# Pausing the adaLN steps in the SSM and MLA part, moving the rotary keys' PSUM read to ScalarE, and giving GpSimd some of the weights' low parts

## The chip, the core and the metric

The kernel runs on one core of one Trainium2 chip. The metric is the device time of one launch in microseconds (us); the time before is the median of three runs. The engines are named as in the profile: PE (matmul), DVE (VectorE), ACT (ScalarE), POOL (GpSimd), SP (SyncE, which here only issues DMAs).

## The reference, cut to what matters

A trunk of two layers over 512 tokens of width 1024. A layer is FFN, token mixer, FFN, each modulated by adaLN columns and followed by a LayerNorm. The mixer has three branches that read the same input:

```python
DEPTH = 2; SEQ = 512; D_MODEL = 1024
ada = (cond @ w_ada[l] + b_ada[l]).reshape(B, 3, 3, D)          # shift, scale, gate of each sub-layer
...
proj = h @ w_in + b_in
q_a, kv_a, k_rope, dil_qkv, u, gate_logits = jnp.split(proj, SPLIT_POINTS, axis=-1)
k_pe = jnp.broadcast_to(rope(k_rope, positions)[:, :, None, :], (B, S, MLA_HEADS, MLA_ROPE_DIM))
y_mla = causal_block_attention(q, k, kv[..., MLA_NOPE_DIM:], ...)  # latent attention (MLA), 8 heads
y_dil = dilated_attention(qkv[:, :, 0], qkv[:, :, 1], qkv[:, :, 2])
y_ssm = jax.nn.gelu(s5_ssm(u, lam_re, lam_im, log_dt, b_re, b_im, c_re, c_im, d_skip))
y_ssm = y_ssm * jax.nn.sigmoid(y_ssm @ w_glu + b_glu)
merged = (gates[:, :, 0] * (y_mla @ w_br[0]) + gates[:, :, 1] * (y_dil @ w_br[1]) + gates[:, :, 2] * (y_ssm @ w_br[2]))
return merged @ w_out
```

## The kernel before, in words

**Weights.** Every large product is done in three f32r matmuls on high and low parts: `wh*xh + wh*xl + wl*xh` (`mm3`, L129 to L131). A chunk of four 128x128 weight tiles comes in by one SP DMA of 256 KB (`wraw`), ACT casts it to its high part (`whi`, L110), and DVE, or POOL while `self.share` is set and the chunk's number is odd, subtracts to the low part (`wlo`, L112). Chunks are numbered through the program; numbers 146 to 180 of layer 0 are the ones spoken of here, 604 and up in layer 1.

**adaLN.** The adaLN matrix isn't multiplied on PE: each column block `araw` is loaded by SP and reduced on DVE (`ada_col`, L183, one custom instruction of 128x512 and a small read of the accumulator). The blocks are spread over the program as jobs: `tick` takes one job from `self.jobs` each time it is called.

**Who sets the order.** The Python order is a priority. A list scheduler with its own cost table places the instructions of each engine's queue; each engine then runs its queue strictly in order and waits at semaphores.

**The mixer's first part** (some 430 to 500 us of layer 0 and 1875 to 1945 us of layer 1) runs four SSM chains `ssm_f` (f = 0 to 3), with the low-rank projections of MLA (`low_rank`) and the dilated values as filling. For each f:

- `ssm_powers` builds the matrices `W` and `C` on POOL by complex products (`cmul`, L536 to L541, 128x64 each), with a scratch tile from `half`;
- ACT copies them into block form (`BD` and `CD`, L697 and L699);
- PE transposes and multiplies them (L732, L739), ACT copies the results (`BT` L734, `T` L743);
- DVE turns the input by phases and scans (`Z` L755 to L760, L765, L767 to L772), and PE takes the result (L779);
- later DVE and ACT compute the gelu (`y` L790, `t` L791 to L794, with a load of an activation table).

In `low_rank`, five products are read out of PSUM by ACT as `raw0` to `raw4` (L1117); the sixth holds the rotary keys, which DVE reads out of PSUM as `kpe` (L1128).

**A shared scratch.** `half` has six buffers that are used in turn (128x256). Among the users are the POOL products of `ssm_powers`, the DVE phases (`ssm_phases`) and four loads of a permutation table for the dilated part (L1241), which are issued as DMAs from ACT's queue:

```python
    def half(self):
        return self.t(self.sb, "half", 6, 256)
...
                for z in range(4):
                    sl = slice(256 * z, 256 * z + 256)
                    pz = self.half()
                    nc.scalar.dma_start(pz, self.A["perm"][:, sl])      # L1241
                    nc.scalar.copy(self.perm[:, sl], pz)
```

A load of the table can be issued once the earlier user of its buffer is done. In Python these loads stand after the MLA part; the scheduler places them earlier, inside the SSM part.

Of the kernel before, what the change touches and what calls it, by code (L numbers as in the profile page):

```python
# [12 lines left out]
AF = mybir.ActivationFunctionType  # L13
ALU = mybir.AluOpType
# [27 lines left out]
class Packer:  # L42


    def __init__(self):
        self.tiles = []
        self.ada = []


class Builder:  # L50
    def __init__(self, nc, tc, ctx, A, pk, plan):
        self.nc, self.tc, self.A, self.pk, self.plan = nc, tc, A, pk, plan
        ep = ctx.enter_context

        self.edge = ep(tc.tile_pool(name="edge", bufs=1, side="right"))
        self.edge.tile([P, 56], F32, name="edge")
        self.const = ep(tc.tile_pool(name="const", bufs=1))
        self.wp = ep(tc.tile_pool(name="wp", bufs=1))
        self.sb = ep(tc.tile_pool(name="sb", bufs=1))
        self.hs = tc.tile_pool(name="hs", bufs=1, space=bass.MemoryType.DRAM)  # L60
        self.hs = ep(self.hs)
        self.ps = ep(tc.tile_pool(name="ps", bufs=8, space=PSUM))
        self.ntile = 0
        self.nada = 0
        self.cur = None
        self.share = False
        self.normed = None
        self.jobs = iter(())
        self.gated = set()
        self.side = iter(())  # L70
        self.uid = 0
# [118 lines left out]

    def tick(self, n=1):
        for _ in range(n):
            next(self.jobs, None)
            with self.behind():
                next(self.side, None)

# [912 lines left out]
    def low_rank(self, p, l, out):  # L1109


        nc = self.nc
        raw = []
        for n in range(5):
            ps = self.gemm([("w_in", (l,), k, n) for k in range(KT)], self.x)
            r = self.t(p, f"raw{n}")
            nc.scalar.activation(r, ps, AF.Identity, bias=self.col(("b_a", l), n))  # L1117
            raw.append(r)
            if n == 2:
                rq = self.rms(l, raw[:3], "q_norm", 384)  # L1120
                next(rq)
            yield
        next(rq)
        rr = 640 + np.arange(32)
        sw = 640 + (np.arange(32) + 16) % 32
        ps = self.gemm([("w_in", (l,), k, np.concatenate([rr, sw, rr, sw])) for k in range(KT)], self.x)
        kpe = self.t(p, "kpe")
        nc.vector.scalar_tensor_tensor(kpe, ps, self.col(("b_kr", l)), self.rope, ALU.add, ALU.mult)  # L1128
        yield
        rk = self.rms(l, raw[3:], "kv_norm", 256)  # L1130
        next(rk)
        yield
        next(rq, None)
        next(rk)
        yield
        ps = self.pst()
        ks = self.t(self.sb, "sq", 2)[:, :P]
        nc.scalar.dma_start(ks, self.A["kpe_sum"])
        nc.tensor.matmul(ps, ks, kpe, start=True, stop=True)
        nc.scalar.copy(kpe, ps)  # L1140
        yield
        next(rk, None)
        kvn = []
        for r in raw[3:]:
            kvn.append(self.pair(p, f"kv{len(kvn)}"))
            self.split(r, *kvn[-1])
        out.update(q=raw[:3], kvn=kvn, kpe=kpe)

    def mixer(self, l, nxt, last, pend):
        nc = self.nc  # L1150
# [3 lines left out]
        def drain(g):  # L1154
            for _ in g:
                pass
        with self.pool("r") as rp:
            with self.pool("u") as up, self.pool("ssm") as sp:
                us = self.project(up, l, pend)
                lr = {}  # L1160

                def values():
                    for g in range(3):
                        for r in self.dil_values(sp, l, g):
                            if r is not None:
                                Vd[g] = r
                            yield
                low = self.low_rank(rp, l, lr)
                val = values()

                def side_work():
                    for _ in range(6):
                        yield next(low)
                    for _ in range(4):
                        next(low, None)
                        yield next(val)
                    yield from val
                fill = side_work()
                chains = [self.ssm_f(sp, l, f, us[f]) for f in range(4)]
                y_ssm = []  # L1180
                glu = self.glu(self.sb, sp, l, us, y_ssm)
                step(chains[0])
                drain(self.ssm_powers(l, 1))
                step(fill)
                step(fill)
                self.ssm_blocks(1)
                for f in range(4):
                    step(chains[f])
                    if f > 0:
                        drain(chains[f - 1])  # L1190
                    if f < 3:
                        self.ssm_phases(f + 1)
                    for _ in range(FILLS[f][0]):
                        step(fill)
                    if f < 3:
                        step(chains[f + 1])
                        if f < 2:
                            drain(self.ssm_powers(l, f + 2))
                    for _ in range(FILLS[f][1]):
                        step(fill)  # L1200
                    step(chains[f])
                    for _ in range(FILLS[f][2]):
                        step(fill)
                    if f < 2:
                        self.ssm_blocks(f + 2)
                drain(fill)
                step(glu)
                drain(chains[3])
                drain(glu)
            self.prep_pool.__exit__(None, None, None)  # L1210
            with self.pool("mla") as mp:
                parts = []
                for r in lr["q"]:
                    parts.append(self.pair(mp, f"n{len(parts)}"))
                    self.split(r, *parts[-1])
                self.mla_mask = self.table(mp, "mla_mask", S)
                for r in self.mla_prepare(mp, l, lr["kvn"], lr["kpe"]):
                    if r is not None:
                        Ks, Vs = r
                y_mla, yb = [], {}  # L1220

                hs = [self.mla_head(mp, l, h, parts, Ks[h], Vs, yb) for h in range(8)]

                for h in range(-3, 9):
                    if h + 3 < 8:
                        step(hs[h + 3])
                    if h >= 2 and h % 2 == 0:
                        y_mla.append(self.mla_values(h // 2 - 1, Vs, yb))
                    if 0 <= h < 8:
                        drain(hs[h])  # L1230
                    if -2 <= h < 6:
                        step(hs[h + 2])
        with self.pool("yd") as yp:
            y_dil = []
            pre = []
            with self.pool("dil") as dp:
# [26 lines left out]
                for hh in range(4):  # L1263
# [2 lines left out]
                        for _ in range((2, 1, 1, 2, 0)[k]):  # L1266
                            step(fill)
                    drain(fill)
            self.tick(99)
            with self.pool("merge") as p:  # L1270
                return self.merge(p, l, (y_ssm, y_mla, y_dil), pre, nxt, last)

# [7 lines left out]
    def merge(self, p, l, ys, pre, nxt, last):  # L1280

        nc = self.nc
        acc = [self.t(p, f"acc{n}") for n in range(KT)]
        for bi, br in enumerate((2, 0, 1)):
            parts = []
            for k, y in enumerate(ys[bi]):
                parts.append(self.pair(p, f"y{k}"))
                self.split(y, *parts[-1])
            for n in range(KT):
                sg = pre[n] if bi == 0 and n < len(pre) else self.gate(p, l, br, n, "sg", 3)  # L1290
                ps = self.gemm([("w_br", (l, br), k, n) for k in range(4)], parts)
                if bi == 0:
                    nc.vector.tensor_tensor(acc[n], sg, ps, ALU.mult)
                else:
                    nc.vector.tensor_tensor(sg, sg, ps, ALU.mult)
                    nc.vector.tensor_tensor(acc[n], acc[n], sg, ALU.add)
        merged = []
        for n in range(KT):
            merged.append(self.pair(p, f"m{n}"))
            self.split(acc[n], *merged[n])  # L1300
        self.new_h()
        for j in range(KT):
            nc.scalar.dma_start(self.H[j], self.hd[j])
        return self.tail(lambda n: [("w_out", (l,), k, n) for k in range(KT)], merged, self.mod[l, 1][2], nxt, last)
# [187 lines left out]
```

## Time and profile before

| what | value |
| --- | --- |
| time before, median of 3 runs | 2906.31 us (2905.78 to 2906.53) |
| profiled execution: its own time | 2904.84 us |
| profiled execution: span from first to last instruction | 2902.7 us |
| mean granted TensorE clock | 0.982 of full speed |
| PE busy in the span | 2804.4 us (97%) |
| DVE / ACT / POOL busy | 1671.0 / 1109.5 / 467.8 us |

The times in the trace are those of the profiled execution, counted from its span's start. PE is nearly always busy, so a change can only win where PE waits, and it loses wherever it makes PE wait more. The matmuls of a 128x512 tile start every 0.22 to 0.23 us at full clock.

### The profile page before, as it was taken

The page shows a single profiled execution, that of the slowest core. Times are in us where ns is not written, and L with a number is a line of the kernel's source. Part 1 is how long each engine was busy: PE and PEld are TensorE (multiplying, and loading weights), DVE is VectorE, ACT ScalarE, POOL GpSimd, SP SyncE. Part 2 cuts the span into 40 slices and gives each one's busy share as a digit, 9 for nine tenths or more (in the row PEclk, how much of TensorE's full clock was granted, in tenths as well). Part 3 has the DMA queues.
Part 4 walks back from the last instruction along what each step waited for, and adds up shares of the span by engine and source line. Part 5 has one row for each costly group of instructions (what it writes and reads, how often), then busy time and mean ns, then how long its engine had stood idle before and what let it go on. Part 6 is the DMA issues. An engine that isn't in the chain of part 4 may idle for free.

```text
span 2902.7 us, 40766 instructions
## 1 busy us (share of the span) xinstructions
PE 2804.4 (97%) x14384; PEld 2375.5 (82%) x14384; DVE 1671.0 (58%) x4234; ACT 1109.5 (38%) x2174; POOL 467.8 (16%) x728
## 2 busy tenths in 40 slices
PE   8999998999999989999999999989999999999997
PEld 6888886978888878888888888869788888888886
DVE  8755469983444465544566554699734444753334
ACT  4333244373443334223343233543643433432332
POOL 2120375000000060000421003840000000600004
PEclk9999999999999999999999999989999999999998
DMA  7545345543234324544244453446422343153331
GB/s 278 168 134 146 112 122 161 184 147 98 84 91 113 98 63 141 153 120 147 87 118 141 135 145 102 145 135 203 142 84 81 97 113 97 58 160 102 96 98 51
DMA packets 205836, 359.38 MB, mean 124 GB/s; under 512 B 23104, under 2 KB 40000, under 8 KB 205632
## 3 DMA queue, kind: packets, MB, share of 16 engines
q1 hardware_dynamic: 198864, 346.32, 39.9%
q10 hardware_dynamic: 6768, 10.47, 1.2%
q8 instruction: 112, 1.84, 0.3%
q14 instruction: 92, 0.75, 0.1%
HBM read 339.92 MB, written 16.78 MB: 123 GB/s over the span
## 4 chain that ended last, share of the span: by engine, by line
PE 84%; DVE 8%; POOL 3%; DMA 2%; ACT 2%; issue 1%; ACTq 0%; DVEq 0%; SPq 0%; POOLq 0%
PE ps L129 26%; PE ps L130 26%; PE ps L131 26%; PE ps L899 1%; DVE wlo L112 1%; DMA araw<-wa 1%; DMA wraw<-ws 1%; DVE lnst L148 1%; DVE araw L183 1%; PE ps L1090 1%; DVE lnst L147 1%; PE ps L316 1%; PE ps L1002 1%; PE ps L1079 0%; PE ps L931 0%
## 5 line engine op out<-in xcount | busy, mean ns | idle before, releaser
L110 ACT CAST whi<-wraw 128x512 fp32r<-128x512 f32 x916 | 563.6, 621 | 1287.8 <-PE ps L130 925.4
L112 DVE TENSOR_TENSOR wlo<-wraw,whi 128x512 fp32r<-128x512 f32 x872 | 608.3, 702 | 733.9 <-ACT whi L110 707.4
L130 PE MATMUL ps<-xl,whi 128*128 128x512 f32 (+1 forms) x2496 | 943.6, 378 | 0.3 <-DVE xl L139 0.3
L129 PE MATMUL ps<-xh,whi 128*128 128x512 f32 (+1 forms) x2496 | 940.0, 379 | 3.3 <-ACT xh L136 3.2
L131 PE MATMUL ps<-xh,wlo 128*128 128x512 f32 (+1 forms) x2496 | 941.6, 378 | 0.0
L129 PEld LDWEIGHTS ps<-xh,whi 128*128 128x128 f32 x2496 | 472.1, 190 | 88.6 <-ACT xh L136 5.0
L131 PEld LDWEIGHTS ps<-xh,wlo 128*128 128x128 f32 x2496 | 472.7, 189 | 85.2
L130 PEld LDWEIGHTS ps<-xl,whi 128*128 128x128 f32 x2496 | 473.3, 190 | 84.2 <-DVE xl L139 0.5
L129 PE MATMUL ps<-gh,whi 128*128 128x512 f32 (+1 forms) x836 | 304.0, 364 | 0.3 <-ACT gh L136 0.3
L130 PE MATMUL ps<-gl,whi 128*128 128x512 f32 (+1 forms) x836 | 301.6, 361 | 0.2 <-DVE gl L139 0.2
L131 PE MATMUL ps<-gh,wlo 128*128 128x512 f32 (+1 forms) x836 | 300.6, 360 | 0.0
L112 POOL TENSOR_TENSOR wlo<-wraw,whi 128x512 fp32r<-128x512 f32 x44 | 58.4, 1328 | 1165.1 <-ACT whi L110 1165.1
L130 PEld LDWEIGHTS ps<-gl,whi 128*128 128x128 f32 x836 | 161.6, 193 | 24.2 <-issue 1.0
L129 PEld LDWEIGHTS ps<-gh,whi 128*128 128x128 f32 x836 | 161.6, 193 | 24.2 <-issue 1.0
L131 PEld LDWEIGHTS ps<-gh,wlo 128*128 128x128 f32 x836 | 161.6, 193 | 22.5
L301 POOL TENSOR_TENSOR H<-H,ln 128x512 f32<-128x512 f32 x6 | 7.8, 1293 | 971.5 <-ACT ln L300 971.5
L439 DVE TENSOR_TENSOR sil<-sil,ps 128x512 f32<-128x512 f32 (+1 forms) x94 | 61.0, 652 | 118.4 <-PE ps L131 113.7
L183 DVE CUSTOM_DVE_ANT_0 araw<-araw,cond,adac 128x512 f32<-128x512 f32 x128 | 96.7, 755 | 14.9 <-DMA araw<-wa 14.2
L183 DVE CUSTOM_DVE_ANT_0 araw<-araw,cond,cols 128x512 f32<-128x512 f32 x128 | 96.7, 755 | 9.8 <-DMA araw<-wa 9.8
L284 DVE SCALAR_TENSOR_TENSOR H<-ps,G,H 128x256 f32<-128x256 f32 (+1 forms) x68 | 40.1, 590 | 80.7 <-PE ps L131 80.7
L129 PE MATMUL ps<-whi,xh 128*128 128x512 f32 x192 | 79.3, 415 | 1.3 <-DVE vst L954 1.3
L130 PE MATMUL ps<-wlo,xh 128*128 128x512 f32 x192 | 77.8, 405 | 0.0
(519 smaller groups left out, 3605.8 us busy)
## 6 DMA issues: line engine op xcount, KB each, us to landing
wraw<-ws SPq DMA_DIRECT2D x916, 256.0 KB, 2.7
araw<-wa SPq DMA_DIRECT2D x256, 256.0 KB, 2.8
raw<-wa SPq DMA_DIRECT2D x16, 512.0 KB, 6.9
vd<-vst SPq DMA_DIRECT2D x24, 256.0 KB, 2.6
V<-vd SPq DMA_DIRECT2D x24, 256.0 KB, 4.6
hd<-H SPq DMA_DIRECT2D x32, 128.0 KB, 1.8
H<-hd ACTq DMA_DIRECT2D x16, 256.0 KB, 3.3
H<-xT SPq DMA_DIRECT2D x8, 256.0 KB, 7.6
```

Source lines behind the costliest of these rows:

```text
L110: nc.scalar.copy(hi, raw)
L112: e.tensor_tensor(lo, raw, hi.bitcast(F32), ALU.subtract)
L129: nc.tensor.matmul(ps, w[0], x[0], start=start, stop=False)
L130: nc.tensor.matmul(ps, w[0], x[1], start=False, stop=False)
L131: nc.tensor.matmul(ps, w[1], x[0], start=False, stop=stop)
L147: nc.vector.scalar_tensor_tensor(t, t, -0.5, v, ALU.mult, ALU.mult)
L148: nc.vector.scalar_tensor_tensor(y, t, 1.5, y, ALU.add, ALU.mult)
L183: self.nc.vector.tensor_tensor_reduce(out=w, in0=w, in1=self.cond[:, k0:k0 + n], scale=1.0, scalar=a if k0 else self.col(("b_ada", l), q), ...
L284: nc.vector.scalar_tensor_tensor(h, ps, G[:, j:j + 1], h, ALU.mult, ALU.add)
L316: self.nc.tensor.matmul(ps, self.ones, dg, start=True, stop=True)
L439: nc.vector.tensor_tensor(s[:, :n], s[:, :n], p3, ALU.mult)
L899: nc.tensor.matmul(s, q[:, P * i:P * i + P], K[:, :w], start=True, stop=True)
```

## The change

Three edits, all in the mixer:

1. `self.hold` is set from after `project` until MLA is done. While it is set, `tick` takes no adaLN job. What is left is taken by `tick(99)`, which moves from ahead of the merge into it.
2. The rotary keys leave PSUM by an ACT activation that adds the bias; DVE then multiplies by the rope table from SBUF. Before, one DVE instruction did both from PSUM.
3. `self.share` is True from the last SSM chain's start until MLA begins, so that the low parts of odd chunks there are made by POOL.

```diff
@@ tick @@
         for _ in range(n):
-            next(self.jobs, None)
+            if not self.hold:
+                next(self.jobs, None)
             with self.behind():
                 next(self.side, None)
@@ low_rank @@
         kpe = self.t(p, "kpe")
-        nc.vector.scalar_tensor_tensor(kpe, ps, self.col(("b_kr", l)), self.rope, ALU.add, ALU.mult)
+        nc.scalar.activation(kpe, ps, AF.Identity, bias=self.col(("b_kr", l)))
+        nc.vector.tensor_tensor(kpe, kpe, self.rope, ALU.mult)
@@ mixer @@
                 us = self.project(up, l, pend)
+
+                self.hold = True
                 lr = {}
...
                         if f < 2:
                             drain(self.ssm_powers(l, f + 2))
+                        else:
+                            self.share = True
...
             self.prep_pool.__exit__(None, None, None)
+            self.share = False
             with self.pool("mla") as mp:
...
+        self.hold = False
         with self.pool("yd") as yp:
...
-            self.tick(99)
             with self.pool("merge") as p:
                 return self.merge(p, l, (y_ssm, y_mla, y_dil), pre, nxt, last)
@@ merge @@
             self.split(acc[n], *merged[n])
+        self.tick(99)
         self.new_h()
```

Line numbers of the changed kernel are larger by one to nine (L1119 there is L1117 before, L1250 is L1241). Since the scheduler places the instructions, the queues are shown at three places.

**ACT's queue in layer 0, while `ssm_powers` of f = 2 runs on POOL.** `raw0` and `raw1` are the first two projections of `low_rank`, `ln0` a norm's scratch, `half_621` the first load of the permutation table. Before:

```order
L1117 ACTIVATE raw0_302_4148<-ps_301_4109,cols_77 128x512 [waits PE_49]
L826 ACTIVATE ln0_315_4320<-raw0_302_4148 128x512 [waits Activation_49]
L110 CAST whi150_4659<-wraw150_4657 128x512 [waits DMAHW0_49,DVE_49]
L110 CAST whi151_4677<-wraw151_4675 128x512 [waits DMAHW1_49,DVE_49,PE_49]
L110 CAST whi152_4711<-wraw152_4709 128x512 [waits DMAHW2_49,DVE_49,PE_49]
L1117 ACTIVATE raw1_304_4190<-ps_303_4150,cols_77 128x512 [waits PE_49]
...
L110 CAST whi155_4911<-wraw155_4909 128x512 [waits DMAHW1_49,PE_49]
L1241 DMA half_621_6605<-perm 128x256 [waits Pool_49]
L1117 ACTIVATE raw3_329_4480<-ps_328_4440,cols_77 128x512 [waits PE_49]
```

And now:

```order
L1119 ACTIVATE raw0_302_4146<-ps_301_4109,cols_77 128x512 [waits PE_49]
L828 ACTIVATE ln0_315_4312<-raw0_302_4146 128x512 [waits Activation_49]
L1250 DMA half_621_6480<-perm 128x256 [waits DMAHW2_49,DVE_49,Pool_49]
L111 CAST whi150_4645<-wraw150_4643 128x512 [waits DMAHW0_49,DVE_49]
L111 CAST whi151_4663<-wraw151_4661 128x512 [waits DMAHW1_49,DVE_49,PE_49]
L111 CAST whi152_4695<-wraw152_4693 128x512 [waits DMAHW3_49,DVE_49,PE_49]
L1119 ACTIVATE raw1_304_4185<-ps_303_4148,cols_77 128x512 [waits PE_49]
```

The first load of the table has moved up in ACT's queue, from behind `whi155` to ahead of `whi150`. In both kernels the count of POOL that it waits for is the one that the last product of `ssm_powers` for f = 2 leaves (L541 before, L543 now, on `C`). Layer 1 has the same move, from behind `whi613` to ahead of `whi608`.

**ACT's queue at the rotary keys, layer 0.** `half_624` is the fourth load of the table, `t2` the gelu. Now:

```order
L1250 DMA half_624_6489<-perm 128x256 [waits DMAHW1_49,Pool_49]
L111 CAST whi160_5128<-wraw160_5126 128x512 [waits PE_49]
L1130 ACTIVATE kpe_347_4679<-ps_346_4642,cols_77 128x512 [waits PE_49]
L793 ACTIVATE t2_311_4209<-y_334_4526 128x512 [waits DMAHW3_49,DMAHW2_49,DMAHW7_49,DMAHW0_49,DVE_49]
L111 CAST whi161_5146<-wraw161_5144 128x512 [waits DMAHW4_49,PE_49]
```

Before, `kpe` isn't in this queue (it stands in DVE's, ahead of `wlo160` and of `y`), and the other four rows stand in the same order. The new row stands behind the fourth load, which waits for POOL, and behind `whi160`.

**POOL's queue behind the last product of `ssm_powers` for f = 3, layer 0.** These rows are new; before, the low parts of these chunks are in DVE's queue:

```order
L113 TENSOR_TENSOR wlo163_5241<-wraw163_5238,whi163_5240 128x512 [waits DMAHW4_49,DVE_49,Activation_49]
L113 TENSOR_TENSOR wlo165_5298<-wraw165_5295,whi165_5297 128x512 [waits DMAHW1_49,DVE_49,Activation_49]
L113 TENSOR_TENSOR wlo167_5375<-wraw167_5372,whi167_5374 128x512 [waits DMAHW5_49,DVE_49,Activation_49]
L113 TENSOR_TENSOR wlo169_5433<-wraw169_5430,whi169_5432 128x512 [waits DMAHW0_49,DVE_49,Activation_49]
L113 TENSOR_TENSOR wlo171_5469<-wraw171_5466,whi171_5468 128x512 [waits DMAHW3_49,DVE_49,Activation_49]
...
L113 TENSOR_TENSOR wlo179_5676<-wraw179_5673,whi179_5675 128x512 [waits DMAHW5_49,DVE_49,Activation_49]
```

Nine low parts of each layer have moved from DVE to POOL, 163 to 179 by twos in layer 0. As for the adaLN blocks, the scheduler places them nearly where they were: ahead of the instruction that makes `kpe`, 62 of them are done before and 60 now; ahead of the last product of MLA (L888 before) 93 in both.

## Rows read from the trace of the kernel before

**Rows 1.** Windows of core 0: busy time per engine, clock, DMA share, GB/s.

```profile
440.00:460.00 20.00, 15.83 (x84) 13.89 (x83) 19.90 (x51) 11.73 (x24) 18.36 (x41) 0.91 0.51 159
460.00:480.00 20.00, 14.62 (x67) 11.80 (x66) 18.67 (x58) 3.63 (x7) 14.61 (x36) 0.86 0.65 191
```

The columns are the window and its length, then busy us (and instructions) of PE, PEld, DVE, ACT and POOL, the granted TensorE clock, the DMA share and GB/s.

**Rows 2.** PE's waits, 430 to 500 us: total, times, longest.

```profile
PE ps L732 <- DVE kpe L1128: 4.8, 1, 4.8
PE ps L739 <- ACT BT L734: 3.1, 1, 3.1
PE ps L779 <- DVE Z L772: 2.4, 1, 2.4
PE ps L779 <- DVE Z L769: 1.7, 1, 1.7
```

**Rows 3.** PE's waits, 500 to 660 us.

```profile
PE ps L899 <- DVE mq L888: 2.2, 1, 2.2
PE ps L129 <- DVE vst L954: 1.3, 1, 1.3
```

**Rows 4.** The chain that ended last, from 438 to 479 us: start, us, what.

```profile
438.79 0.63 ACT whi L110
...
453.24 0.78 DVE Z L772
...
478.05 0.63 ACT whi L110
```

**Rows 5.** Timeline of ACT, layer 0: start, us, instruction, idle before and releaser.

```profile
434.57 0.63 ACT L826 ACTIVATE ln<-raw 128x512 f32<-128x512 f32 x1
...
439.31 0.68 ACT L1117 ACTIVATE raw<-ps,cols 128x512 f32<-128x512 f32 x1
...
452.80 0.33 ACTq L1241 DMA_DIRECT2D half<-perm  x1
453.18 0.69 ACT L1117 ACTIVATE raw<-ps,cols 128x512 f32<-128x512 f32 x1 [2.52 <-POOL C L541]
```

**Rows 6.** Timeline of POOL, layer 0.

```profile
420.68 0.29 POOL L539 TENSOR_TENSOR W<-ssmq,W 128x64 f32<-128x64 f32 x1
...
426.83 0.32 POOL L541 TENSOR_TENSOR C<-C,half 128x64 f32<-128x64 f32 x1
...
434.73 0.62 POOL L537 TENSOR_TENSOR half<-ssmq,W 128x64 f32<-128x64 f32 x1
435.31 0.29 POOL L539 TENSOR_TENSOR W<-ssmq,W 128x64 f32<-128x64 f32 x1
...
452.12 0.65 POOL L541 TENSOR_TENSOR C<-C,half 128x64 f32<-128x64 f32 x1
```

**Rows 7.** Timeline of DVE, layer 0.

```profile
432.29 2.91 DVE L112 TENSOR_TENSOR wlo<-wraw,whi 128x512 fp32r<-128x512 f32 x4 [11.72 <-ACT whi L110]
...
440.05 0.68 DVE L755 TENSOR_TENSOR Z<-ps,Ec 128x512 f32<-128x512 f32 x1
...
476.97 0.74 DVE L1128 SCALAR_TENSOR_TENSOR kpe<-ps,cols,rope_t 128x512 f32<-128x512 f32 x1
```

**Rows 8.** Timeline of ACT, layer 1.

```profile
1878.09 0.63 ACT L826 ACTIVATE ln<-raw 128x512 f32<-128x512 f32 x1
```

**Rows 9.** Timeline of POOL, layer 1.

```profile
1878.84 0.29 POOL L539 TENSOR_TENSOR W<-ssmq,W 128x64 f32<-128x64 f32 x1
...
1895.32 0.65 POOL L541 TENSOR_TENSOR C<-C,half 128x64 f32<-128x64 f32 x1
```

**Rows 10.** Timeline of DVE, layer 1.

```profile
1883.29 0.68 DVE L755 TENSOR_TENSOR Z<-ps,Ec 128x512 f32<-128x512 f32 x1
```

**Rows 11.** The page's costliest groups: busy, mean ns, idle before.

```profile
L112 DVE TENSOR_TENSOR wlo<-wraw,whi 128x512 fp32r<-128x512 f32 x872 | 608.3, 702 | 733.9 <-ACT whi L110 707.4
L112 POOL TENSOR_TENSOR wlo<-wraw,whi 128x512 fp32r<-128x512 f32 x44 | 58.4, 1328 | 1165.1 <-ACT whi L110 1165.1
```

**Rows 12.** PE's waits, layer 1, 1945 to 2105 us.

```profile
PE ps L899 <- DVE mq L888: 2.1, 1, 2.1
```

More of the change, by code (lines that the diff above doesn't have):

```diff
@@ L1232, in mixer @@
                         step(hs[h + 2])
+        self.hold = False
         with self.pool("yd") as yp:
```

## The prediction

> **What bounds the kernel now.** I read PE's waits first, then the chain that ended last, then the queues of ACT, POOL and DVE over the same stretch. PE fills nearly the whole span except in the SSM part of each layer, and there in one short stretch: in the two windows from 440 to 480 us it is busy 15.83 and 14.62 of 20 us and its clock falls to 0.91 and 0.86 of full speed [rows 1]. The waits that make this up are few: `Z` of the second SSM chain (1.7 and 2.4 us), the rotary keys (4.8 us) and `BT` (3.1 us) [rows 2]. Further on, in MLA, PE waits only 2.2 us for `mq` and 1.3 us for `vst` [rows 3]; layer 1 has 2.1 us [rows 12]. So the edits have few us to win, and the question is what they move on the chain of the SSM part. That chain runs through exactly the instructions which the change reorders: the cast at 438.79 (`whi152`), DVE's low part and `Z` until 453.24, later POOL's products, then the cast at 478.05 (`whi160`) [rows 4]. ACT is hardly busy there, but its queue is in order, so what stands ahead of `whi152` decides when `Z` can start.
>
> **The moved table load: a new wait of 10 us in each layer.** Before, ACT ends the norm `ln0` at 434.57 + 0.63 = 435.20 and casts `whi150` to `whi152`, the last of them at 438.79 [rows 4, 5]. Now the first load of the permutation table stands between `ln0` and `whi150`. It waits for the last product of `ssm_powers` (f = 2), which before starts at 452.12 and ends at 452.77 [rows 6]. Before, the same load went out at 452.80, and ACT had stood idle for 2.52 us, released by that very product [rows 5]: a DMA of ACT's queue which waits holds up everything behind it. It cost little there, since most casts were ahead of it. Now behind it are three casts, `raw1` and all that follows; on DVE the low parts `wlo150` to `wlo152` and, behind them in the order, the phases `Z`; on PE the products that wait for `raw1`'s PSUM and for the weights.
>
> How long is the wait? From 435.31 there are 38 of them to the last one (the first and the last of them in [rows 6]). Before, they took until 452.77, since DVE works beside them, and a product then takes 0.62 us and more in place of 0.29 [rows 6]. Now DVE has nothing to do while ACT stands, for its next instruction is `wlo150`. The nearest row for that is the stretch ahead: DVE was idle for 11.72 us up to 432.29 [rows 7], and in it POOL's 20 products from 420.68 to 426.83 + 0.32 = 427.15 took 6.47 us, or 0.324 us each [rows 6]. So 38 x 0.324 = 12.3 us, and the last ends at 435.31 + 12.3 = 447.6. The bounds are that and before's pace, 452.77; I take 447.6, because DVE's idleness follows from the order. From the product's end to ACT's next instruction there were 453.18 - 452.77 = 0.41 us [rows 5, 6]. Then three casts at the pace of casts back to back (0.53 us, estimated from the 0.52 us between `whi152` at 438.79 and ACT's next at 439.31 [rows 4, 5]): `whi152` starts at 448.0 + 1.06 = 449.1. From `whi152` to `Z` there were 440.05 - 438.79 = 1.26 us [rows 4, 7], so `Z` starts at 450.3, **10.3 us later** than 440.05. In layer 1, `ln0` ends at 1878.72 [rows 8], 38 products from 1878.84 end at 1891.1 instead of 1895.32 + 0.65 = 1895.97 [rows 9], `Z` starts at 1893.8 instead of 1883.29 [rows 10]: **10.5 us**. With POOL at before's pace it would be 15.4 in each.
>
> Does PE feel all of it? PE already waits at the end of this chain, for `Z`, 1.7 and 2.4 us [rows 2], so nothing there absorbs it. Its other work is too short to hide 10 us: it comes to stand for `raw1` first, then for `Z`. After `Z` all depends on PE, ACT's copies and POOL's next products in turn [rows 4], so I let the rest of the chain move along. Two more idle stretches of PE in each layer may lower its clock; before, windows with 4 to 5 us of idleness had 0.91 and 0.86 [rows 1]. I add 0.5 us per layer, between 0 and 1.8 (20 us at another 0.09).
>
> [...]
>
> **Rotary keys.** DVE's `kpe` ran from 476.97 to 477.71 and PE waited 4.8 us for it [rows 2, 7]. ACT's read stands behind the fourth table load and `whi160` at 478.05 [rows 4], so it can't start before about 478.6 and ends near 479.3, some 1.5 us later in this chain. PE then meets its wait of 3.1 us for `BT` [rows 2] with that much less slack; but `BT` itself comes behind one more ACT read and one more DVE multiply (about 0.7 us). Part of that is filled by products that PE now has left over. I put it at nothing, between -4.8 us (the wait goes and nothing else is late) and +1.5 us. If the 3.1 us for `BT` weren't there, 1.5 us would show.
>
> **The pause.** The order shows the adaLN blocks almost where they were, 60 in place of 62 ahead of `kpe`, so DVE is spared two blocks there. Nothing, or at most the 1.7 us of `Z`'s first wait [rows 2].
>
> **Low parts on POOL.** Nine subtractions of 0.70 us leave DVE per layer, 6.3 us of its work, and take 1.33 us each on POOL [rows 11], which is idle there; its low parts come 0.6 us later than DVE's, but the weights are made ahead. What DVE gives back can only show where PE waits for DVE: 2.2 + 1.3 us in layer 0 and 2.1 us in layer 1 [rows 3, 12], as well as some small ones. I take 2.3 us per layer, between 0 and 3.5.
>
> **Sum**, against the profiled execution (2904.84 us): 10.3 + 10.5 (stalls) + 1.0 (clock) - 4.6 (low parts) = +17.2, so 2922.0 us. The median of the runs is 1.5 us above that execution, hence **2923.5 us**. A measurement of this kernel can tell about 0.2%, 5.8 us, from no change.
>
> **Rivals.**
>
> *Fuller stall.* POOL keeps its old pace. Against it speak the rows of the stretch with an idle DVE; for it, that other traffic than DVE's may slow it. Stalls 2 x 15.4: 2904.84 + 30.8 + 1 - 4.6 + 1.5 = 2933.5 us.
>
> *Partly absorbed.* The chain loses 10 us at `Z`, but PE's later wait for the rotary keys shrinks, since SP's loads of weights and adaLN blocks go on while ACT stands, and what came late for the next step is there in time. Of 4.8 us a layer [rows 2] at most all goes: 2923.5 - 9.6 = 2914 us.
>
> *Faster.* The table load finds its buffer free, or ACT's queue passes it, so that the casts come at 435.8 as before. The place is ACT's queue behind `ln0`; it decides whether POOL's last product is done by 435.2, where before it ended at 452.77 [rows 5, 6]. Then the gains remain: the rotary keys' 4.8 us and the low parts' 2.3 in each layer, 2 x 7.1: 2906.3 - 14 = 2892 us. Against it: the row of before in which the same load held ACT for 2.52 us.
>
> [...]
>
> *It does nothing.* The scheduler undoes the pause, the rotary keys are covered by the next wait, and the stall is met by equal gains: 2906 us. The stall would have to be below some 5 us per layer, so POOL's last product done by about 442; at 0.29 us each, the shortest in the rows, 38 products from 435.31 end at 446.3 [rows 6].
>
> **Chances.** Full forecast (stalls near 10 us each) 0.50, fuller stall 0.20, partly absorbed 0.18, faster 0.07, nothing 0.05. So slower 0.88, within 0.2% 0.05, faster 0.07. The range takes in the absorbed case with the low parts' full gain (2914 - 2.4 = 2911) and the fuller stall with the clock's upper end and no gain from low parts (2933.5 + 4.6 + 2.6 = 2941, cut to 2938): 2911 to 2938 us, which leaves out the last two cases and a little at the top.
>
> **What would show it.** In the changed kernel's trace ACT should have a wait of some 12 us ended by POOL's `C` product near 447.6 us, with the table load behind it, and again near 1891; POOL's products at about 0.3 us in it; PE idle some 6 us ahead of the products on `whi148` and again ahead of `Z` (L779), together about 10 us more than before; `kpe`'s wait on PE longer, not gone; `mq` shorter. I am wrong if the load goes out before 440 us, if POOL's pace differs, or if the waits after 460 us shrink by more than a few us.

## The result, and the profile after

| | before | changed |
| --- | --- | --- |
| median | 2906.42 us (2905.78 to 2906.93, 4 runs) | 2939.51 us (2938.08 to 2942.65, 4 runs) |
| span of the profiled execution | 2902.7 us | 2936.5 us |
| mean granted clock | 0.982 | 0.980 |

The change makes the kernel slower: ratio 1.0115, 95% interval 1.0099 to 1.0131, which is 33 us. The forecast was 17 us slower, 2923.5 us, with 2911 to 2938 us as its range. The sign was right, and so were the place and the size of the stall; the term for the low parts on POOL was not, and with it the size of the whole.

First the stall. These are rows of ACT's, POOL's and DVE's timelines of the changed kernel in layer 0, one fence for each:

```profile
433.49 0.63 ACT L828 ACTIVATE ln<-raw 128x512 f32<-128x512 f32 x1
446.32 0.33 ACTq L1250 DMA_DIRECT2D half<-perm  x1
446.76 1.66 ACT L111 CAST whi<-wraw 128x512 fp32r<-128x512 f32 x3 [12.63 <-POOL C L543]
```

```profile
435.08 0.29 POOL L542 TENSOR_TENSOR half<-ssmq,W 128x64 f32<-128x64 f32 x1
...
445.98 0.32 POOL L543 TENSOR_TENSOR C<-C,half 128x64 f32<-128x64 f32 x1
```

```profile
447.40 1.89 DVE L113 TENSOR_TENSOR wlo<-wraw,whi 128x512 fp32r<-128x512 f32 x3 [12.59 <-ACT whi L111]
449.22 0.68 DVE L757 TENSOR_TENSOR Z<-ps,Ec 128x512 f32<-128x512 f32 x1
```

ACT stands for 12.63 us, released by POOL's product; the table load goes out at 446.32, and the three casts follow at once. Before, the same casts came between 435.79 and 438.79. POOL runs at 0.29 to 0.32 us per product all the way, while DVE stands for 12.59 us too, and `Z` begins at 449.22 instead of 440.05 [rows 7]. Layer 1 has the same row of ACT:

```profile
1905.49 1.66 ACT L111 CAST whi<-wraw 128x512 fp32r<-128x512 f32 x3 [12.63 <-POOL C L543]
```

PE's waits of the changed kernel in 425 to 520 us of layer 0, which answer to [rows 2], and behind them the two windows that show the cost. The first answers to a window of [rows 1]; in the second, PE before was busy for 16.89 us at a clock of 0.88:

```profile
PE ps L734 <- ACT kpe L1130: 6.9, 1, 6.9
PE ps L130 <- ACT raw L1119: 5.7, 1, 5.7
PE ps L781 <- DVE Z L771: 4.5, 2, 3.7
PE ps L781 <- DVE Z L774: 2.1, 1, 2.1
PE ps L741 <- ACT BT L736: 1.3, 1, 1.3
```

```profile
440.00:460.00 20.00, 11.45 (x41) 8.79 (x40) 11.57 (x24) 10.95 (x22) 8.66 (x26) 0.83 0.28 85
480.00:500.00 20.00, 11.74 (x98) 8.82 (x97) 15.59 (x39) 9.16 (x17) 6.46 (x17) 0.66 0.49 146
```

The waits for `raw` (5.7 us) and for the first `Z` (3.7 us, the longest of its two, instead of 1.7) are the stall as PE sees it. The wait for the rotary keys is longer, 6.9 instead of 4.8 us, and that for `BT` shorter, 1.3 instead of 3.1.

The rest is lost later. PE's queue has the same number of instructions in both kernels, 14,384, so wherever both have the same product at a number, its two starts can be compared. Number 2,200 (a product behind `Z`) comes at 456.6 us before and 466.2 after, 9.6 us late; number 2,370 (behind the waits for the keys and for `BT`) at 489.7 and 499.7, 10.0 us late, near the forecast; number 3,100, in MLA, at 630.9 and 647.0, **16.1 us** late. In between, the prediction had a gain of 2.3 us. Layer 1 goes the same way: PE is 13.6 us late ahead of its stall (number 9,350), 26.3 behind it (9,450) and 34.3 in MLA (10,300). PE's wait for `mq`, which the prediction expected to be shorter, is longer, 2.9 us in layer 0 instead of 2.2 [rows 3]:

```profile
PE ps L901 <- DVE mq L890: 2.9, 1, 2.9
```

Between 490 and 580 us of layer 0 the group of POOL's low parts reads as follows in the changed kernel:

```profile
L113 POOL TENSOR_TENSOR wlo<-wraw,whi 128x512 fp32r<-128x512 f32 x9 | 15.0, 1668 | 65.2 <-ACT whi L111 58.7 <-DVE lnst L145 6.5
```

They take 1.67 us on average, where POOL's low parts before took 1.33 [rows 11]. And this is what stands on DVE beside one of them; POOL's row first, then DVE's:

```profile
545.74 1.29 POOL L113 TENSOR_TENSOR wlo<-wraw,whi 128x512 fp32r<-128x512 f32 x1 [6.86 <-ACT whi L111]
```

```profile
545.57 0.19 DVE L539 TENSOR_TENSOR half<-ssmq,Es 128x32 f32<-128x32 f32 x1
545.68 0.18 DVE L541 TENSOR_TENSOR Es<-ssmq,Es 128x32 f32<-128x32 f32 x1
545.80 1.28 DVE L540 TENSOR_TENSOR Ec<-Ec,half 128x32 f32<-128x32 f32 x1
547.00 0.74 DVE L184 CUSTOM_DVE_ANT_0 araw<-araw,cond,cols 128x512 f32<-128x512 f32 x1
```

The two DVE products of 128x32 just ahead take 0.18 to 0.19 us; the one beside POOL's instruction takes 1.28 us, and ends at 547.08, just behind the end of POOL's instruction at 547.03. It is no wait in the profile; it is a longer instruction. Of the 18 low parts in both layers, 14 have a DVE instruction beside them that is longer by 0.25 us or more than is usual for its form, by 13.9 us in all.

### The profile page after: what moved, and what is told of

The parts are those of the page before. It is cut to its first block, busy times and chain, and to the rows that moved or that the text cites. A ratio compares the mean times of both kernels' runs of the same rounds, so it can differ in the third digit from the quotient of the medians.

```text
span 2936.5 us, 40764 instructions
## 1 busy us (share of the span) xinstructions
PE 2809.7 (96%) x14384; PEld 2376.8 (81%) x14384; DVE 1671.1 (57%) x4216; ACT 1110.0 (38%) x2176; POOL 490.1 (17%) x746
## 4 chain that ended last, share of the span: by engine, by line
PE 80%; DVE 11%; POOL 4%; DMA 2%; ACT 2%; issue 1%; SPq 0%; ACTq 0%; DVEq 0%; POOLq 0%
PE ps L130 25%; PE ps L131 25%; PE ps L132 25%; DMA araw<-wa 2%; DVE wlo L113 1%; PE ps L901 1%; DVE araw L184 1%; DVE Y L767 1%; POOL half L539 1%; DVE lnst L149 1%; POOL half L542 1%; DVE lnst L148 1%; PE ps L1092 1%; DVE lnst L147 1%; PE ps L1004 0%
## 5 line engine op out<-in xcount | busy, mean ns | idle before, releaser
L113 DVE TENSOR_TENSOR wlo<-wraw,whi 128x512 fp32r<-128x512 f32 x854 | 595.6, 703 | 725.0 <-ACT whi L111 708.0
L130 PEld LDWEIGHTS ps<-xh,whi 128*128 128x128 f32 x2496 | 471.5, 189 | 102.0 <-ACT raw L1119 13.4
L113 POOL TENSOR_TENSOR wlo<-wraw,whi 128x512 fp32r<-128x512 f32 x62 | 88.7, 1431 | 1150.2 <-ACT whi L111 1129.4
L132 PE MATMUL ps<-whi,xl 128*128 128x512 f32 x192 | 77.3, 404 | 0.0
```

Of the source, the lines that this page charges most:

```text
L113: e.tensor_tensor(lo, raw, hi.bitcast(F32), ALU.subtract)
L130: nc.tensor.matmul(ps, w[0], x[0], start=start, stop=False)
L132: nc.tensor.matmul(ps, w[1], x[0], start=False, stop=stop)
```

## The experiments

Theory A, formed on the two traces: the pause moves the table load, which costs the stall (some 20 us), and the low parts on POOL hold DVE and cost the rest; the rotary keys cost nothing. Rival B: all of it comes from the pause and what follows from it, and POOL's low parts are harmless. Rival C: the rotary keys cost. Each kernel was timed against the kernel before in runs of the same chip; the ratios are to those runs.

**The pause alone**

```diff
+                self.hold = True      # after project; tick then takes no adaLN job
...
+        self.hold = False             # after MLA; tick(99) moves into merge
```

> Only the pause of the adaLN steps, on the kernel before; the order has the first table load ahead of whi150 as in the whole change. Theory A (the pause moves the load, which costs the stall; the low parts on POOL cost the rest): stall of 10 to 12 us in each layer, 2906 + 20 to 24 = 2926 to 2930 us, and no loss behind 500 us of layer 0. Rival B (all of the loss comes from the pause and what follows from it, the low parts cost nothing): about 2939 us, with 5 us lost between 500 and 620 us of layer 0.

Measured: 2928.72 us against 2905.33, ratio 1.0082 (1.0067 to 1.0097). ACT's timeline of this kernel has the stall of the whole change:

```profile
446.30 0.33 ACTq L1246 DMA_DIRECT2D half<-perm  x1
446.73 1.14 ACT L111 CAST whi<-wraw 128x512 fp32r<-128x512 f32 x2 [12.65 <-POOL C L543]
```

PE is 10.0 us late behind it at number 2,200 and stays so: 9.9 us at number 3,100. So in layer 0 the pause makes the stall and nothing of the 6 us that the whole change loses after it; in layer 1 it makes 2.3 of 8.0 us. Theory A holds for this part.

**The rotary keys alone**

```diff
-        nc.vector.scalar_tensor_tensor(kpe, ps, self.col(("b_kr", l)), self.rope, ALU.add, ALU.mult)
+        nc.scalar.activation(kpe, ps, AF.Identity, bias=self.col(("b_kr", l)))
+        nc.vector.tensor_tensor(kpe, kpe, self.rope, ALU.mult)
```

> Only the rotary keys' read by ACT. Theory A: the read comes some 1.5 us later behind the fourth table load, which the wait for BT hides: 2906 us, within 3 us. Rival C (the keys cost): PE's wait for them grows from 4.8 to over 6 us and nothing gives it back, 2909 to 2912 us. If the edit did what it says and nothing else was late, 2897 us.

Measured: 2907.28 us against 2905.33, ratio 1.0006 (0.9997 to 1.0016): no difference that can be told, and no gain. PE's waits of this kernel, 430 to 510 us:

```profile
PE ps L732 <- ACT kpe L1128: 7.3, 1, 7.3
PE ps L739 <- ACT BT L734: 2.2, 1, 2.2
```

The wait for the keys grows by 2.5 us, that for `BT` shrinks by 0.9 [rows 2].

**The low parts alone**

```diff
+                        else:
+                            self.share = True     # from the last SSM chain
...
+            self.share = False                    # before MLA
```

> Only the low parts of odd chunks on POOL from the last SSM chain to MLA; the order of ACT's table loads is that of the kernel before. Theory A: nine POOL instructions of 1.3 us or more hold DVE for about 1.1 us each and save it 0.7, and what DVE makes comes later: 2912 to 2918 us. Rival B: 2906 us, within 3 us. My prediction's term: 2901.7 us (4.6 us faster).

Measured: 2919.26 us against 2905.33, ratio 1.0049 (1.0034 to 1.0064): 13.9 us slower. The third edit loses three times what it was forecast to win. Beside 14 of its 18 low parts a DVE instruction is longer, by 13.8 us in all.

**The whole change, table loads late**

```diff
-        nc.scalar.copy(kpe, ps)
+        self.kc = nc.scalar.copy(kpe, ps).ins
...
-                    nc.scalar.dma_start(pz, self.A["perm"][:, sl])
+                    with self.tc.issue_after(self.kc):
+                        nc.scalar.dma_start(pz, self.A["perm"][:, sl])
```

> The whole change, but the four table loads are put behind ACT's copy of the rotated keys (after the last SSM products on POOL of that part), so that no cast stands behind them. Theory A: the stall goes, 2939 - 20 to 24 us, and the wait of whi160 for POOL goes too, another 0 to 8 us: 2908 to 2919 us; ACT's wait of 12.6 us is gone. Rival B (the load is not what costs; POOL, DVE or the clock would be): 2930 us or more.

Measured: 2916.64 us against 2905.33, ratio 1.0040 (1.0025 to 1.0055), 22.9 us less than the whole change. ACT's row of 12.63 us is gone: the casts wait 1.44 us for a weight's load.

```profile
436.98 1.37 ACT L111 CAST whi<-wraw 128x512 fp32r<-128x512 f32 x2 [1.44 <-DMA wraw<-ws]
```

PE's wait for the keys is gone from its list too, but that for `BT` stands there instead:

```profile
PE ps L741 <- ACT BT L736: 8.1, 1, 8.1
```

Before, the two were 4.8 + 3.1 = 7.9 us [rows 2]. The wait changes its name and not its size.

**POOL beside, order unchanged**

```diff
             e.tensor_tensor(lo, raw, hi.bitcast(F32), ALU.subtract)
+            if self.odd and c % 2:     # odd chunks, where the change sets share
+                nc.gpsimd.tensor_tensor(self.scrap, raw, hi.bitcast(F32), ALU.subtract)
```

> The kernel before, with its order unchanged on PE, DVE, ACT and SP; where the change gives POOL a low part, POOL makes a second one into an unused tile that nobody reads (nine per layer), while DVE still makes the real one. So DVE gains nothing, its order is the same, and no one waits for POOL's result; only what POOL does beside DVE is new. Theory A (POOL's low parts hold DVE): 18 holds of about 1.0 us on DVE, of which most reach PE between 500 and 600 us: 2912 to 2922 us. Rival B (the cost of the third edit comes from the new order or from low parts that are late, not from holding): 2905 us, within 3 us.

Measured: 2915.95 us against 2904.99, ratio 1.0043 (1.0028 to 1.0058): 11.0 us slower, with the same instructions in the same order on PE, DVE, ACT and SP. Only POOL's 18 instructions are new, and nobody waits for their result. (One cast of ACT in each layer does wait 1.8 us for the end of such an instruction, which still reads the buffer that the cast writes; the kernel with POOL as a copy, further on, has no such wait.) POOL's row and DVE's beside it:

```profile
504.19 1.72 POOL L115 TENSOR_TENSOR W<-wraw,whi 128x512 f32<-128x512 f32 x1 [8.07 <-ACT whi L111]
```

```profile
504.70 1.26 DVE L540 TENSOR_TENSOR half<-ssmq,Es 128x32 f32<-128x32 f32 x1
505.88 0.18 DVE L542 TENSOR_TENSOR Es<-ssmq,Es 128x32 f32<-128x32 f32 x1
```

Again 1.26 us for what takes 0.18. All in all DVE's instructions beside POOL's are longer by 15.8 us. On PE this comes out in part where it waits for DVE; its waits of this kernel in 500 to 660 us, to be read beside [rows 3]:

```profile
PE ps L132 <- DVE vst L957: 3.9, 1, 3.9
PE ps L902 <- DVE mq L891: 2.2, 1, 2.2
PE ps L319 <- DVE lndg L314: 1.5, 1, 1.5
```

The wait for `vst` was 1.3 us before, that for `lndg` 0.5. Theory A holds; the rival that only the order or late low parts cost does not.

**DVE's relief alone.** Nine low parts per layer are left out, and PE takes the high part in their place.

```diff
-            e.tensor_tensor(lo, raw, hi.bitcast(F32), ALU.subtract)
+            if self.odd and c % 2:
+                lo = hi
+            else:
+                e.tensor_tensor(lo, raw, hi.bitcast(F32), ALU.subtract)
```

> The kernel before without the low parts of those odd chunks at all (nine per layer; PE takes the high part in their place, so that its work is the same and that share of the weights' precision is left out). It is the most that the third edit can give back by relieving DVE. My prediction's term says 4.6 us faster than before, 2901 us; if PE's waits for DVE there don't shrink, 2905 us; if the new order costs, 2908 us or more, which would take part of the blame off the holding.

Measured: 2902.25 us against 2904.99, ratio 0.9993 (0.9984 to 1.0002): 2.7 us less, not clear of zero. Even if POOL's work cost nothing, the relief would bring at most 4.6 us (2904.99 x 0.0016, the end of the interval), which is what the prediction took for its likely value.

**The change without the third edit, loads late**

The pause and the rotary keys' read by ACT stay in; the loads are put late as above:

```diff
-                    nc.scalar.dma_start(pz, self.A["perm"][:, sl])
+                    with self.tc.issue_after(self.kc):
+                        nc.scalar.dma_start(pz, self.A["perm"][:, sl])
```

> The change without its third edit, with the four table loads behind the copy of the rotated keys. Theory A, by adding what was measured: 2916.6 - 13.9 = 2902.7 us, 2898 to 2906. If the effects of the edits depend on each other, above 2906 us.

Measured: 2907.04 us against 2904.99, ratio 1.0006 (0.9996 to 1.0015). That is 4 us more than the sum gave: in this company the low parts cost 2916.64 - 2907.04 = 9.6 us, and 13.9 alone. Each of these figures is good to about 4 us, so whether the effects overlap isn't shown.

**The kernel before, loads late**

The loads are put late as above, in the kernel before:

```diff
-                    nc.scalar.dma_start(pz, self.A["perm"][:, sl])
+                    with self.tc.issue_after(self.kc):
+                        nc.scalar.dma_start(pz, self.A["perm"][:, sl])
```

> The kernel before with the four table loads behind the copy of the rotated keys, nothing else. ACT no longer stands behind POOL for 2.5 us near 453 and for 4.8 us near 478 in each layer; the cast of whi160 was on the chain there. Theory A: PE's wait for BT gets shorter, 2 to 4 us per layer: 2897 to 2902 us. Rival (these waits are hidden): 2905 us, within 2 us.

Measured: 2903.71 us against 2904.99, ratio 1.0000 (0.9990 to 1.0009). The theory was wrong here: PE's wait for `BT` falls from 3.1 to 2.1 us, but it waits longer for the first `Z`, 2.9 us in two waits instead of 1.7 in one, and no gain can be told.

**POOL beside, in quarters**

```diff
-                nc.gpsimd.tensor_tensor(self.scrap, raw, hi.bitcast(F32), ALU.subtract)
+                for z in range(4):
+                    q = slice(P * z, P * z + P)
+                    nc.gpsimd.tensor_tensor(self.scrap[:, q], raw[:, q], hi[:, q].bitcast(F32), ALU.subtract)
```

> As the kernel with POOL beside (order on PE, DVE, ACT and SP that of before; POOL makes a second low part that nobody reads), but each is made in four instructions of 128x128. If a hold lasts for one POOL instruction and DVE gets in between two of them, no DVE instruction is held for more than about 0.4 us, and the cost falls to less than half of 11 us: 2907 to 2911 us. If POOL keeps DVE out for all four, or they follow too closely, the holds add up to as much: 2915 us or more.

Measured: 2918.09 us against 2905.41, ratio 1.0045 (1.0030 to 1.0060). Shorter pieces don't help. POOL's group of four and DVE beside it:

```profile
503.16 2.26 POOL L117 TENSOR_TENSOR W<-wraw,whi 128x128 f32<-128x128 f32 x4 [6.48 <-issue]
```

```profile
503.67 0.45 DVE L542 TENSOR_TENSOR half<-ssmq,Es 128x32 f32<-128x32 f32 x1
504.04 0.18 DVE L544 TENSOR_TENSOR Es<-ssmq,Es 128x32 f32<-128x32 f32 x1
504.14 0.41 DVE L153 SCALAR_TENSOR_TENSOR lnst<-lnst 128x4 f32<-128x4 f32 x1
```

DVE does get in between two quarters, but every second of its instructions is held, by some 0.26 us.

**POOL beside, as a copy**

```diff
-                nc.gpsimd.tensor_tensor(self.scrap, raw, hi.bitcast(F32), ALU.subtract)
+                nc.gpsimd.tensor_copy(self.scrap, raw)
```

> As the kernel with POOL beside, but POOL only copies the weight chunk into the unused tile (one input instead of two, 0.8 us by the cast of the same size). If any POOL instruction that reads and writes these tiles holds DVE for its duration, holds of about 0.5 us: 2908 to 2912 us. If only one with two inputs does, 2905 us within 3 us, and no DVE instruction longer than usual beside a copy.

Measured: 2909.93 us against 2905.41, ratio 1.0016 (1.0007 to 1.0026): 4.5 us. The copy takes 0.61 us and holds DVE by about 0.4:

```profile
503.08 0.62 POOL L115 COPY W<-wraw 128x512 f32<-128x512 f32 x1 [9.97 <-DMA wraw<-ws]
```

```profile
503.10 0.63 DVE L539 TENSOR_TENSOR Ec<-ssmq,Ec 128x32 f32<-128x32 f32 x1
```

In all its holds come to 4.6 us, and no engine is seen to wait for one of these copies. So one input less, in half the time on POOL, makes the hold shorter, but doesn't remove it: 4.6 us of holds cost 4.5 us, 15.8 us of them cost 11.0.

**The pause with late loads**

The loads are put late as above, in the kernel with the pause alone:

```diff
-                    nc.scalar.dma_start(pz, self.A["perm"][:, sl])
+                    with self.tc.issue_after(self.kc):
+                        nc.scalar.dma_start(pz, self.A["perm"][:, sl])
```

> Only the pause, with the four table loads behind the copy of the rotated keys: the stall by itself is the difference to the pause alone (2928.7 us). Theory A: 20 to 23 us less, 2905 to 2909 us; the pause itself then brings nothing that can be measured. If the pause had a gain that the stall covers up, below 2900 us.

Measured: 2905.52 us against 2905.41, ratio 0.9999 (0.9990 to 1.0008). The stall by itself is 2928.72 - 2905.52 = **23.2 us**, and the pause without it is worth nothing that can be measured.

**The mirror: POOL's result is used, DVE makes the spare one**

```diff
-            e.tensor_tensor(lo, raw, hi.bitcast(F32), ALU.subtract)
+            e.tensor_tensor(self.scrap if self.odd and c % 2 else lo, raw, hi.bitcast(F32), ALU.subtract)
+            if self.odd and c % 2:
+                nc.gpsimd.tensor_tensor(lo, raw, hi.bitcast(F32), ALU.subtract)
```

> The mirror of the kernel with POOL beside: POOL makes the real low part of those odd chunks, and DVE makes a second one into the unused tile, so that DVE's order is that of before, it is held as there and gains nothing, but PE has to wait for POOL's result. What it takes over 2915.95 us (POOL beside) is the price of low parts that come late. If PE's weights are made far enough ahead, 2916 us within 3 us, and the 5.6 us of the third edit that holding (11.0) and relief (-2.7) don't explain come from its new order on DVE and PE; if lateness costs, 2919 to 2923 us.

Measured: 2919.58 us against 2906.17, ratio 1.0047 (1.0031 to 1.0064), beside 1.0043 (1.0028 to 1.0058) for POOL beside. Each against the kernel before in its own runs, that is 13.4 us beside 11.0, but the intervals overlap almost wholly, so this doesn't tell whether late low parts cost anything.

## Why the prediction was right in its sign and too small

**The moved table load: right, in place, mechanism and size.** Forecast 10.3 + 10.5 us and 1.0 for the clock, 21.8 in all; measured 23.2 us, as the pause alone less the pause with late loads. No run tells the clock's part from the rest. The steps can be checked one by one. POOL's last product was to end at 447.6 and ended at 446.30 (445.98 + 0.32), since its products were at 0.29 to 0.32 us and all that led up to them came earlier. From there to ACT's cast it took 0.46 us, where 0.41 was taken. `Z` was to start at 450.3 and started at 449.22; behind it DVE then waited 1.02 us for an adaLN block, and PE was late by 9.6 us at number 2,200 and by 10.0 at number 2,370. In layer 1 the stall makes PE later by 12.7 us (26.3 - 13.6), where 10.5 was forecast; in the kernel with the pause alone it is 10.9. The rival with POOL at its old pace did not come about, nor did the one in which PE's wait for the keys absorbs part of it: with all three edits that wait grew, and with the pause alone it fell from 4.8 to 3.4 us in layer 0, but PE is still 9.6 us late at number 2,370.

**The rotary keys: right.** Nothing was forecast; alone they give 2 us more, with -0.9 to +4.6 us as the interval. PE's wait for them got longer, as worked out (by 2.5 us, not 1.5), and most of what was meant to be won stands in the wait for `BT`, which was seen directly where the loads are late.

**The pause: right.** The scheduler undoes it, but for the place of the table load.

**The low parts on POOL: this step failed.** The prediction said: "What DVE gives back can only show where PE waits for DVE", 2.3 us per layer, "between 0 and 3.5". Measured, the edit costs 13.9 us alone and 9.6 us in company, instead of -4.6. Both ends of the bound were on the side of a gain, which assumed that an instruction on an idle POOL costs DVE nothing. The runs show that it holds DVE: with order and results unchanged, 18 POOL instructions that nobody needs cost 11.0 us. Against 18 low parts that DVE is spared, at about 0.6 us each (three take 1.89 us above), or 11 us, stand holds of 13.8 us: DVE comes out with less time than before.

That step also broke with one of the prediction's own. For the stall it took POOL's pace from rows in which a POOL product is longer beside a busy DVE, 0.62 us instead of 0.29 [rows 6], but only in that direction, to say how fast POOL is without DVE; what POOL's work does to DVE beside it was not asked. The trace of the changed kernel shows it: POOL's low part runs from 545.74 to 547.03, and a DVE product that usually takes 0.19 us ends at 547.08. The trace of before already holds such rows: beside 20 of the 44 low parts that POOL makes there, a DVE instruction is longer by 0.25 us or more. A DVE and a POOL row of before, near 343 us of layer 0:

```profile
342.78 1.83 DVE L112 TENSOR_TENSOR wlo<-wraw,whi 128x512 fp32r<-128x512 f32 x1 [3.96 <-ACT whi L110]
```

```profile
342.76 1.31 POOL L112 TENSOR_TENSOR wlo<-wraw,whi 128x512 fp32r<-128x512 f32 x1
```

DVE's low part takes 1.83 us beside POOL's and 0.70 us on average [rows 11]. With 1.1 us a hold, 18 holds and 11 us of relief, the term would have had bounds from a gain of some us to a loss of about 9, and at that end its sum would have been 2923.5 + 4.6 + 9 = 2937 us, near the 2939.5 measured.

**What stays open.** Of the 13.9 us, POOL's work beside DVE explains 11.0 and the relief -2.7, or 8.3 together. The other 5.6 us may come from low parts that are late or from the new order on DVE and PE. By its median the mirror kernel would put 2.4 us of them (13.4 - 11.0) on lateness, but each of these figures is good to about 4 us, so neither share is told from nothing. By adding, the parts of the whole change are 23.2 (stall) + 2.0 (keys) + 9.6 (low parts in company) = 34.8 us, and 33 were measured.

None of the kernels is faster than the one before by more than its interval.

## What to carry to other kernels

A change of priorities reaches queues that it doesn't name (here ACT's casts stood for 12.63 us behind a table load that waited for POOL): look in each engine's queue for an instruction that waits for another engine, ask what now stands behind it, and time that other engine's last instruction. Work given to an idle engine need not be free for the busy one (here 18 POOL subtractions that nobody needs cost 11.0 us): look in the trace of before for the same pair side by side, and compare the busy engine's durations there with its usual ones, since a hold showed here as a longer instruction (1.28 us for what takes 0.19) and in no list of waits. Give a cost that no row has been looked up for a bound on both sides of zero.

## What the runs showed of the hardware

- Beside a POOL subtraction of 128x512 with two inputs (1.29 us beside an idle DVE, at 351.12 us of the kernel before), a DVE instruction was held: in the kernel with POOL beside, 13 of them by 1.0 to 1.1 us and three by 0.5 to 0.8. For three sizes of DVE's own instruction the hold was much the same: there 0.18 us became 1.26 us for 128x32 and 0.41 became 1.54 for 128x256, and in the kernel before 0.70 became 1.83 for 128x512.
- In the kernel with POOL in quarters, subtractions of 128x128 held DVE by about 0.26 us each, several times (0.45 us for what takes 0.19), and cost as much as one of 128x512 (12.7 and 11.0 us for 18 chunks, the intervals overlap).
- In the kernel with POOL as a copy, the copy of the same tile took 0.61 us and held DVE by about 0.4 us (0.63 us for what takes 0.19), and 18 of them cost 4.5 us.
- POOL's instructions were longer too: the nine low parts of layer 0 in the changed kernel took 1.67 us on average beside a busy DVE, against the 1.29 us beside an idle one; a POOL product of 128x64 took 0.62 us beside a busy DVE (434.73 us of the kernel before) and 0.29 to 0.32 beside one that stood (435.08 to 446.30 of the changed one).
